# Gated outputs turned by block transposes on VectorE instead of 128x128 transposes on TensorE: one core, a hybrid GLA/HGRN2 layer

## The chip, the cores and the metric

The kernel runs on one core of one Trainium2 chip. The metric is device time in microseconds (us), the median of several runs. TensorE (PE in the profile; PEld is its weight load) does matmuls, VectorE (DVE) and ScalarE (ACT) elementwise work, GpSimd (POOL) a little of it, and SyncE (SP) issues nearly all transfers between main memory and the on-chip memory SBUF, each as one instruction on one in-order queue. In the text p is the time from one issue to the next on that queue for the small transfers that the change adds.

## The reference, cut to what matters

```python
p = jnp.einsum('btd,de->bte', h, w_in)                 # h: normalised, modulated x
...
o_a, s_a = chunked_gla(...)                            # 4 heads x 128 = 512 columns
o_h, s_h = chunked_gla(...)                            # 4 heads x 128 = 512 columns
o_a = rms_norm(o_a, g_on_gla).reshape(B, T, GLA_V) * jax.nn.silu(z_a)
o_h = rms_norm(o_h, g_on_hgrn).reshape(B, T, HGRN_W) * jax.nn.silu(z_h)
o = jnp.einsum('bte,ed->btd', jnp.concatenate([o_a, o_h], axis=-1), w_out)
y = x + gate[:, None] * rms_norm(o, g_post)
```

4096 prompt frames and 64 sample frames, model width 1024. The change touches only the way from `o_a` and `o_h` to the product with `w_out`.

## The kernel before, in words

The work is done in three stages. Stage one projects the frames for the GLA heads and runs their recurrence, group by group of 256 frames; stage two does the same for the HGRN2 heads. Both leave their normalised outputs in scratch memory, `oa_d` (already times its gate) and `oh_d` (not yet), one piece of 128 frames by 512 columns per tile. Stage three (`phase3`, from line 1218) has 33 tiles: 32 of 128 prompt frames and, as the seventh, one of 64 sample frames. For each tile it does the following.

- `load` (1229) fetches the two halves of the tile into `og` (two buffers) by `og_load` (1211), and the rows of x into `xt`, all on SP's queue.
- `turn` (1241) multiplies the second half by its gate `e` (1244; here called the gating), turns the tile by eight TensorE transposes of 128x128 (1252) into the PSUM tiles `ps_tp` and `ps_ms`, and splits the result by `split` (84) into a rounded part `ogh` on ScalarE (87) and a rest `ogl` on VectorE (88). The matmul needs frames along the free dimension and columns on the partitions, hence the turning.
- The output projection (1287) runs 48 matmuls of 512 columns: two output halves q, eight column blocks kt, three terms of hi and lo. The weights of kt 0 to 3 are tiles `wv`, those of kt 4 to 7 are `wu`.
- ScalarE squares the sum (1292), VectorE multiplies by the gate row (1296), does a Newton iteration for the reciprocal root (71 to 81, twelve tiny instructions), adds x (1299), and SP stores y (1303).

The gate `e` of a later tile comes from another projection, `z_tile` (1185): 24 matmuls (571) into `ps_at`, a sigmoid (1193) and a product (1194). A generator runs it some tiles ahead, so that 24 z matmuls stand beside the 48 of each output tile until the last five tiles, which have none. Its input `hf` is loaded by SP (527), four loads for two tiles, and split on ScalarE and VectorE (90, 91).

Within these, a scheduler in the framework sets the order on each engine when the program is built; an engine then runs its list in order. Every transfer has one of eight semaphores in turn, so that a transfer is issued only when the eighth before it has landed.

Of the kernel before, what the change touches and what calls it, by code (L numbers as in the profile page):

```python
# [6 lines left out]
F32 = mybir.dt.float32  # L7
# [4 lines left out]
ALU = mybir.AluOpType  # L12
# [3 lines left out]
P = 128  # L16
D = 1024
# [11 lines left out]
class Kernel:  # L29
# [1180 lines left out]

    def og_load(self, tile, og):

        g, j, (kind, _, r, _) = tile
        g = g if kind == "p" else -1
        self.nc.sync.dma_start(og[:r, :512], self.oa_d[g][j])
        self.nc.sync.dma_start(og[:r, 512:], self.oh_d[g][j])

    def phase3(self, tiles, zgen, og):
        nc, t = self.nc, self.t
        with ExitStack() as s:  # L1220
            one = self.pool(s, "p3one")
            ap = self.pool(s, "p3a")
            gg = one.tile([P, 2, D], F32, name="gg")
            for i in range(2):
                nc.sync.dma_start(gg[:, i, :], self.gate_d[i : i + 1, :].to_broadcast([P, D]))
            Wo = self.W3["o"]
            og0 = og

            def load(i):
                g, j, (kind, r0, r, o) = tiles[i]  # L1230
                if i > 0:
                    og = ap.tile([P, D], F32, name="og", bufs=2)
                    self.og_load(tiles[i], og)
                else:
                    og = og0
                xt = self.xp.tile([P, D], F32, name="xt", bufs=2)
                src = t["x_prompt"] if kind == "p" else t["x_sample"]
                nc.sync.dma_start(xt[:r], src[0, r0 : r0 + r, :])
                return og, xt

            def turn(i, og):
                r = tiles[i][2][2]
                e = self.zq.pop(0)
                nc.vector.tensor_tensor(og[:r, 512:], og[:r, 512:], e, ALU.mult)
                hi = ap.tile([P, D], F32R, name="ogh", bufs=2).rearrange("p (k c) -> p k c", k=KT)
                lo = None
                if r == P:
                    lo = ap.tile([P, D], F32R, name="ogl", bufs=2).rearrange("p (k c) -> p k c", k=KT)
                for q, tag in enumerate(("tp", "ms")):
                    pt = self.ps(tag).rearrange("p (k c) -> p k c", k=4)  # L1250
                    for k in range(4):
                        nc.tensor.transpose(
                            pt[:, k, :r], og[:r, (4 * q + k) * P : (4 * q + k + 1) * P], self.ident[:r, :r]
                        )
                    ks = slice(4 * q, 4 * q + 4)
                    self.split(hi[:, ks, :r], lo[:, ks, :r] if r == P else hi[:, ks, r : 2 * r], pt[:, :, :r], gain=self.col[:, 50 + q : 51 + q])
                return hi, lo

            n = len(tiles)
            og, xt = load(0)  # L1260
            next(zgen, None)
            hl = turn(0, og)
            for i in range(n):
                g, j, (kind, r0, r, o) = tiles[i]
                dst = t["y_prompt"] if kind == "p" else t["y_sample"]
                x_now, (hi, lo) = xt, hl
                if i + 1 < n:
                    next(zgen, None)
                    og, xt = load(i + 1)
                    hl = turn(i + 1, og)  # L1270
                cnd = 0 if kind == "p" else 1
                ss = self.small.tile([P, 2], F32, name="y_ss")[:r]
                y = ap.tile([P, D], F32, name="y", bufs=2)
                if i == n - 1:

                    self.tc.keep_in_program_order(nc.scalar.preload_act_table_set("natural_log_exp_and_others"))
                for q in range(2):
                    po = self.ps("pj")
                    cs = slice(512 * q, 512 * q + 512)
                    m = 0  # L1280
                    for kt in range(KT):
                        wh, wl = Wo[2 * kt + q][:, 0], Wo[2 * kt + q][:, 1]
                        if r < P:
                            self.pair_step(po, hi[:, kt, : 2 * r], r, wh, wl, kt)
                            continue
                        for a, b in ((hi, wh), (hi, wl), (lo, wh)):
                            nc.tensor.matmul(po[:r], a[:, kt, :r], b, start=m == 0, stop=m == 3 * KT - 1)  # L1287
                            m += 1
                    if r < P:
                        self.fold(po, r, 512, y[:, cs])  # L1290
                    junk = ap.tile([P, 512], mybir.dt.bfloat16, name="sq", bufs=1)[:r]
                    nc.scalar.activation(junk, po[:r], AF.Square, accum_out=ss[:, q : q + 1])  # L1292
                    if q:
                        nc.vector.tensor_tensor(ss[:, 0:1], ss[:, 0:1], ss[:, 1:2], ALU.add)
                        rs = self.rstd(ss[:, 0:1], D, table=i == n - 1)
                    nc.vector.tensor_tensor(y[:r, cs], po[:r], gg[:r, cnd, cs], ALU.mult)
                for q in range(2):
                    cs = slice(512 * q, 512 * q + 512)
                    nc.vector.scalar_tensor_tensor(y[:r, cs], y[:r, cs], rs, x_now[:r, cs], ALU.mult, ALU.add)
                    if i == n - 1:  # L1300
                        (nc.scalar if q else nc.sync).dma_start(dst[0, r0 : r0 + r, cs], y[:r, cs])
                if i < n - 1:
                    nc.sync.dma_start(dst[0, r0 : r0 + r, :], y[:r])
# [189 lines left out]
```

## Time and profile before

| what | us |
|---|---|
| median of 3 runs | 2168.07 (2166.62 to 2170.9) |
| profiled execution, own time | 2167.58 |
| profiled execution, span of the core | 2165.8 |
| PE busy in the span | 2121.3 (98%) |
| output tile with z matmuls, start to start | 17.30 |
| last matmul of stage three ends at | 2158.26 |

The times in the profile's rows run from the span's start. A row of the timeline reads: start, length, engine, line, operation, output<-inputs, count, and in brackets how long the engine had been idle before it and what ended that. SPq is SP's queue: the length is the time that the issuing instruction took, not the transfer's. A row of the chain of waits reads: start, length, engine, tile, line, count.

### The profile page before, as it was taken

What the parts mean: (1) busy time and instruction counts of PE and PEld (TensorE: products, weight loads), DVE (VectorE), ACT (ScalarE), POOL (GpSimd) and SP (SyncE); (2) the same over time, 40 slices, a digit from 0 to 9 for tenths busy, and PEclk for the clock granted to TensorE, in tenths of its full rate; (3) what the DMA queues carried; (4) which work ended last, traced back from release to release, by engine and by line L of the source; (5) the groups of instructions that cost most, each with busy time, mean ns of one, the idle gap of its engine ahead of it and who ended that gap; (6) DMA issues with size and microseconds to landing.
All of it is one profiled execution on the core that took longest, in us unless ns stands there. A gap on an engine that the chain in (4) does not pass through costs nothing.

```text
span 2165.8 us, 44469 instructions
## 1 busy us (share of the span) xinstructions
PE 2121.3 (98%) x16776; PEld 1868.9 (86%) x16776; DVE 1448.8 (67%) x4735; ACT 979.4 (45%) x2790; POOL 237.1 (11%) x636
## 2 busy tenths in 40 slices
PE   7999999999999999999999999999989999999998
PEld 6898899999999888889899988999868888888887
DVE  6866666666666687777778877677894454545444
ACT  5665555655556564434444444444542222222212
POOL 3200010000110111110111111000230000000000
PEclk9999999999999999999999999999999999999999
DMA  9321111211111231011121111001343433333322
GB/s 269 118 76 55 55 50 60 79 55 55 50 60 65 89 102 42 30 40 58 58 70 46 35 31 50 31 31 42 99 151 119 127 128 107 127 112 131 109 102 87
DMA packets 98706, 173.15 MB, mean 80 GB/s; under 512 B 12668, under 2 KB 34656, under 8 KB 98492
## 3 DMA queue, kind: packets, MB, share of 16 engines
q1 hardware_dynamic: 98348, 170.05, 24.1%
q8 instruction: 132, 2.16, 0.4%
q14 instruction: 82, 0.67, 0.1%
q10 hardware_dynamic: 144, 0.26, 0.0%
HBM read 118.35 MB, written 51.93 MB: 79 GB/s over the span
## 4 chain that ended last, share of the span: by engine, by line
PE 86%; DVE 7%; ACT 3%; DMA 3%; issue 1%; POOL 0%; SPq 0%; DVEq 0%; ACTq 0%; POOLq 0%
PE ps_pj L571 22%; PE ps_pj L559 22%; PE ps_pj L1287 16%; PE ps_at L571 7%; PE ps_at L908 2%; PE ps_ms L791 2%; PE ps_at L638 2%; PE ps_o L775 2%; PE ps_o L770 2%; DMA xt<-in_x_prompt_dram 2%; DVE wst L861 1%; PE ps_tp L506 1%; PE ps_at L718 1%; PE ps_tp L745 1%; PE ps_pj L579 1%
## 5 line engine op out<-in xcount | busy, mean ns | idle before, releaser
L571 PE MATMUL ps_pj<-wu,hh 128*128 128x512 f32 x1632 | 405.3, 397 | 3.3 <-DVE hh L91 2.4
L559 PE MATMUL ps_pj<-hh,wu 128*128 128x256 f32 (+1 forms) x2976 | 395.6, 287 | 0.0
L559 PEld LDWEIGHTS ps_pj<-hh,wu 128*128 128x128 f32 x2976 | 373.8, 191 | 4.6 <-issue 0.3
L571 PEld LDWEIGHTS ps_pj<-wu,hh 128*128 128x128 f32 x1632 | 297.6, 188 | 65.5 <-issue 3.5
L559 PE MATMUL ps_pj<-hh,wv 128*128 128x256 f32 (+1 forms) x1536 | 214.1, 289 | 0.0
L559 PEld LDWEIGHTS ps_pj<-hh,wv 128*128 128x128 f32 x1536 | 192.5, 188 | 14.9 <-issue 12.9
L571 PE MATMUL ps_pj<-wv,hh 128*128 128x264 f32 x1464 | 203.2, 290 | 1.6 <-DVE wv L91 1.6
L571 PEld LDWEIGHTS ps_pj<-wv,hh 128*128 128x128 f32 x1464 | 184.5, 188 | 6.5 <-issue 3.1
L1292 ACT ACTIVATE sq<-ps_pj 128x512 bf16<-128x512 f32 (+1 forms) x66 | 39.4, 597 | 294.7 <-PE ps_pj L1287 289.7
L1287 PE MATMUL ps_pj<-wv,ogh 128*128 128x512 f32 x512 | 163.0, 399 | 0.0
L571 PE MATMUL ps_at<-wu,hh 128*128 128x512 f32 x672 | 158.5, 392 | 0.0
L1287 PE MATMUL ps_pj<-wu,ogh 128*128 128x512 f32 x512 | 157.9, 390 | 0.0
L90 ACT CAST hh<-hf 128x512 fp32r<-128x512 f32 (+1 forms) x188 | 117.7, 626 | 75.2 <-PE ps_pj L571 36.8
L571 PEld LDWEIGHTS ps_at<-wu,hh 128*128 128x128 f32 x672 | 126.9, 189 | 26.4
L91 DVE TENSOR_TENSOR hh<-hf,hh 128x512 fp32r<-128x512 f32 (+1 forms) x188 | 133.1, 710 | 14.2 <-ACT hh L90 12.8
L1153 ACT ACTIVATE g<-ps_pj 128x256 f32<-128x256 f32 (+1 forms) x128 | 49.4, 386 | 198.2 <-PE ps_pj L559 197.7
L861 DVE TENSOR_TENSOR wst<-wst,T 128x160 f32<-128x160 f32 (+4 forms) x480 | 118.1, 263 | 4.0
L1287 PEld LDWEIGHTS ps_pj<-wu,ogh 128*128 128x128 f32 x512 | 96.1, 188 | 20.7
L890 POOL COPY T<-T 128x16 f32<-128x16 f32 (+1 forms) x32 | 9.6, 299 | 942.3 <-DVE Qg L831 870.4
L1287 PEld LDWEIGHTS ps_pj<-wv,ogh 128*128 128x128 f32 x512 | 94.4, 189 | 19.1
L1287 PE MATMUL ps_pj<-wv,ogl 128*128 128x512 f32 x256 | 100.7, 394 | 0.0
L1287 PE MATMUL ps_pj<-wu,ogl 128*128 128x512 f32 x256 | 99.7, 390 | 0.0
(300 smaller groups left out, 3705.7 us busy)
## 6 DMA issues: line engine op xcount, KB each, us to landing
xt<-in_x_prompt_dram SPq DMA_DIRECT2D x64, 512.0 KB
hf<-h_d SPq DMA_DIRECT2D x128, 256.0 KB
h_d<-hf SPq DMA_DIRECT2D x64, 256.0 KB
out_y_prompt_dram<-y SPq DMA_DIRECT2D x31, 512.0 KB
wst<-in_w_in_dram SPq DMA_DIRECT2D x36, 256.0 KB
ada_st<-in_w_ada_dram SPq DMA_DIRECT2D x32, 256.0 KB
oa_d<-e SPq DMA_DIRECT2D x32, 256.0 KB
oh_d<-e SPq DMA_DIRECT2D x32, 256.0 KB
```

The source lines that it names most:

```text
L90: self.nc.scalar.copy(hi, src)
L91: (eng or self.nc.vector).tensor_tensor(lo, src, hi.bitcast(F32), ALU.subtract)
L559: self.nc.tensor.matmul(ps[:, :T], a, b, start=i == 0, stop=i == n - 1)
L571: self.nc.tensor.matmul(ps[:r, : c1 - c0], a, b, start=kt == 0 and i == 0, stop=kt == KT - 1 and i == 2)
L638: nc.tensor.transpose(pt[:, i * P : (i + 1) * P], D[:, c + i, :], self.ident)
L770: nc.tensor.matmul(po[h], A[:, c * 4 + h, :], v, start=h < n, stop=St is None and h == 4 - n)
L775: nc.tensor.matmul(o, Q[rows[s], c * G + g, :], St[rows[s], g, :], start=NS == 2 and not apart and h == 1, stop=h == 4 - NS or h == 3 and ...
L791: nc.tensor.matmul(pd[s * w : (s + 1) * w, g, :], kc[:CL, g, s * w : (s + 1) * w], vs[c][:CL, h * P : (h + 1) * P], start=not apart, stop= ...
L861: nc.vector.tensor_tensor(parts(dst), parts(src), t.unsqueeze(3).to_broadcast(shape), ALU.mult)
L908: nc.tensor.matmul(pas[s][rows, g0 + g], K[rr, 2 * pr + g, rows], Yt[rr, o : o + P], start=True, stop=True)
L1153: nc.scalar.activation(sg, pf[:, :T], AF.Sigmoid)
L1287: nc.tensor.matmul(po[:r], a[:, kt, :r], b, start=m == 0, stop=m == 3 * KT - 1)
```

## The change

The tile is no longer turned by TensorE. Instead every half of it (512 columns) is loaded so that its columns already lie by quarters of partitions: partitions 32a to 32a+31 take the a-th group of 32 columns of every column block, 32 frames at a time. For one half that is 16 transfers of 32 partitions, 4 runs of 32 numbers (128 bytes) each, 16 KB in all. VectorE then transposes 32x32 blocks (`nc.vector.transpose`, STREAM_TRANSPOSE in the orders below), which completes the turn, and the split reads SBUF where it read PSUM.

The GLA half comes from main memory in this layout (16 loads for one before). The HGRN2 half is loaded as before, gated on VectorE, and then laid out by 16 more transfers from SBUF to SBUF into `oq`, half of a staging buffer (`wst`). `og` is loaded two tiles ahead, the gating stands in the middle of the tile before last, and the transposes one tile ahead. A 128-frame tile so has 32 small transfers and one ordinary one where it had two.

```diff
     def og_load(self, tile, og):
-        self.nc.sync.dma_start(og[:r, :512], self.oa_d[g][j])
+        src = self.oa_d[g][j].rearrange("(b t) (k a i) -> a b t k i", t=32, a=4, i=32)
+        for a in range(4):
+            for b in range(r // 32):
+                self.nc.sync.dma_start(self.quarter(og, a, b), src[a, b])
         self.nc.sync.dma_start(og[:r, 512:], self.oh_d[g][j])
+
+    @staticmethod
+    def quarter(t, a, b):
+        return t[32 * a : 32 * a + 32, b * P : b * P + P].rearrange("p (k i) -> p k i", i=32)
...
+            def gate(i, og):
+                r = tiles[i][2][2]
+                nc.vector.tensor_tensor(og[:r, 512:], og[:r, 512:], self.zq.pop(0), ALU.mult)
+                oq = self.wst()
+                for a in range(4):
+                    for b in range(r // 32):
+                        src = og[32 * b : 32 * b + 32, 512:].rearrange("p (k a i) -> p a k i", a=4, i=32)[:, a]
+                        nc.sync.dma_start(self.quarter(oq, a, b), src)
+                return og, oq
...
-                for q, tag in enumerate(("tp", "ms")):
-                    pt = self.ps(tag).rearrange("p (k c) -> p k c", k=4)
-                    for k in range(4):
-                        nc.tensor.transpose(
-                            pt[:, k, :r], og[:r, (4 * q + k) * P : (4 * q + k + 1) * P], self.ident[:r, :r]
-                        )
+                for q, src in enumerate(ogs):
                     ks = slice(4 * q, 4 * q + 4)
-                    self.split(hi[:, ks, :r], lo[:, ks, :r] if r == P else hi[:, ks, r : 2 * r], pt[:, :, :r], gain=self.col[:, 50 + q : 51 + q])
+                    oT = ap.tile([P, 512], F32, name="oT", bufs=1)[:, : 4 * r].rearrange("p (k c) -> p k c", k=4)
+                    nc.vector.transpose(
+                        oT.rearrange("p k (b t) -> p b k t", t=32),
+                        src[:, : 4 * r].rearrange("p (b k i) -> p b k i", k=4, i=32),
+                    )
+                    self.split(hi[:, ks, :r], lo[:, ks, :r] if r == P else hi[:, ks, r : 2 * r], oT, gain=self.col[:, 50 + q : 51 + q])
...
+            ogs = [gate(0, og)]
+            og = load(1)
+            hl = turn(0, ogs.pop(0))
+            next(zgen, None)
+            ogs.append(gate(1, og))
             for i in range(n):
                 if i + 1 < n:
                     next(zgen, None)
-                    og, xt = load(i + 1)
-                    hl = turn(i + 1, og)
+                    xt = load_x(i + 1)
+                    if i + 2 < n:
+                        og = load(i + 2)
+                    hl = turn(i + 1, ogs.pop(0))
...
+                    if q == 0 and i + 2 < n:
+                        ogs.append(gate(i + 2, og))
```

The order on SP's queue in the middle of stage three, before, two tiles (the last number of a scratch tile's name only numbers it; `oa_d_0_137` is the GLA half of a tile, `oh_d_0_139` its HGRN2 half):

```order
L1303 DMA out_y_prompt_dram<-y 128x1024
L1238 DMA xt<-in_x_prompt_dram 128x1024
L1215 DMA og<-oa_d_0_137 128x512
L1216 DMA og<-oh_d_0_139 128x512
L527 DMA hf<-h_d_151 128x512 x2
L1303 DMA out_y_prompt_dram<-y 128x1024
L1238 DMA xt<-in_x_prompt_dram 128x1024
L527 DMA hf<-h_d_151 128x512
```

And in the changed program, from the load of the same tile on:

```order
L1219 DMA og<-oa_d_0_137 32x4x32 x16
L1220 DMA og<-oh_d_0_139 128x512
L1332 DMA out_y_prompt_dram<-y 128x1024
L1245 DMA xt<-in_x_prompt_dram 128x1024
L1256 DMA wst<-og 32x4x32 x16
L1219 DMA og<-oa_d_1_138 32x4x32 x16
L1220 DMA og<-oh_d_1_140 128x512
L1332 DMA out_y_prompt_dram<-y 128x1024
L527 DMA hf<-h_d_156 128x512 x2
L1256 DMA wst<-og 32x4x32 x16
L527 DMA hf<-h_d_156 128x512 x2
```

Each tile's 16 transfers into `wst`, which wait for its gating, stand behind the loads of that very tile and ahead of the loads of the next.

On VectorE before, around the end of an output tile (1296 are its two halves out of PSUM, 1244 the gating of the next tile):

```order
L1296 TENSOR_TENSOR y<-ps_pj,gg 128x512
L1244 TENSOR_TENSOR og<-og,e 128x512
L1294 TENSOR_TENSOR y_ss<-y_ss 128x1
L1296 TENSOR_TENSOR y<-ps_pj,gg 128x512
L71 TENSOR_SCALAR y_ss<-y_ss 128x1
```

And after, with the numbers of the buffers (`y_23118` is one output tile; `og_22930` and `wst_22834` are the two halves of the next one; some rows of the Newton iteration are between the two pieces):

```order
L1325 TENSOR_TENSOR y_23118<-ps_pj_23119,gg_21801 128x512
L1323 TENSOR_TENSOR y_ss_23117<-y_ss_23117 128x1
L1325 TENSOR_TENSOR y_23118<-ps_pj_23165,gg_21801 128x512
L1269 STREAM_TRANSPOSE oT_23109<-og_22930 128x4x4x32
L1251 TENSOR_TENSOR og_22930<-og_22930,e_22296 128x512
...
L1328 SCALAR_TENSOR_TENSOR y_23118<-y_23118,nwt_y_23193,xt_22928 128x512 x2
L1269 STREAM_TRANSPOSE oT_23113<-wst_22834 128x4x4x32
L88 SCALAR_TENSOR_TENSOR ogl_23108<-oT_23113,col_168,ogh_23107 128x512
```

The gating of a tile now stands behind the last half of the tile before it, and both transposes of a tile stand there too, the second one behind the transfers that follow the gating.

On TensorE the eight transposes of each tile stood between the 24 z matmuls and the 48 of the tile:

```order
L571 MATMUL ps_at<-wu,hh 128x512 x24
L1252 MATMUL ps_tp<-ident,og 128x128 x4
L1252 MATMUL ps_ms<-ident,og 128x128 x4
L1287 MATMUL ps_pj<-wv,ogh 128x512 x2
L1287 MATMUL ps_pj<-wv,ogl 128x512
```

They are gone. The 48 are now split by halves of the turned tile, first the 24 of `wv` for both output halves, later the 24 of `wu`; in one tile of two all 24 z matmuls stand between the two halves, in the other 12 stand there and 12 ahead of the tile:

```order
L1314 MATMUL ps_pj<-wv,ogh 128x512 x2
L1314 MATMUL ps_pj<-wv,ogl 128x512
L571 MATMUL ps_at<-wu,hh 128x512 x24
L1314 MATMUL ps_pj<-wu,ogh 128x512 x4
L1314 MATMUL ps_pj<-wu,ogl 128x512
```

More of the change, by code (lines that the diff above doesn't have):

```diff
@@ L1226, in phase3, with load_x @@
             Wo = self.W3["o"]
-            og0 = og
             def load(i):
+                og = ap.tile([P, D], F32, name="og", bufs=2)
+                self.og_load(tiles[i], og)
+                return og
+            def load_x(i):
                 g, j, (kind, r0, r, o) = tiles[i]
[L1231 to L1235, printed above, removed]
                 xt = self.xp.tile([P, D], F32, name="xt", bufs=2)
@@ L1238, in load, with turn @@
                 nc.sync.dma_start(xt[:r], src[0, r0 : r0 + r, :])
-                return og, xt
-            def turn(i, og):
+                return xt
+            def gate(i, og):
                 r = tiles[i][2][2]
-                e = self.zq.pop(0)
-                nc.vector.tensor_tensor(og[:r, 512:], og[:r, 512:], e, ALU.mult)
+                nc.vector.tensor_tensor(og[:r, 512:], og[:r, 512:], self.zq.pop(0), ALU.mult)
[5 more added lines that the diff above has]
+                return og, oq
+            def turn(i, ogs):
+                r = tiles[i][2][2]
                 hi = ap.tile([P, D], F32R, name="ogh", bufs=2).rearrange("p (k c) -> p k c", k=KT)
@@ L1248, in turn @@
                     lo = ap.tile([P, D], F32R, name="ogl", bufs=2).rearrange("p (k c) -> p k c", k=KT)
-                for q, tag in enumerate(("tp", "ms")):
-                    pt = self.ps(tag).rearrange("p (k c) -> p k c", k=4)
-                    for k in range(4):
-                        nc.tensor.transpose(
-                            pt[:, k, :r], og[:r, (4 * q + k) * P : (4 * q + k + 1) * P], self.ident[:r, :r]
-                        )
-                    ks = slice(4 * q, 4 * q + 4)
-                    self.split(hi[:, ks, :r], lo[:, ks, :r] if r == P else hi[:, ks, r : 2 * r], pt[:, :, :r], gain=self.col[:, 50 + q : 51 + q])
+                for q, src in enumerate(ogs):
+                    ks = slice(4 * q, 4 * q + 4)
+                    oT = ap.tile([P, 512], F32, name="oT", bufs=1)[:, : 4 * r].rearrange("p (k c) -> p k c", k=4)
[3 more added lines that the diff above has]
+                    )
+                    self.split(
+                        hi[:, ks, :r], lo[:, ks, :r] if r == P else hi[:, ks, r : 2 * r], oT,
+                        gain=self.col[:, 50 + q : 51 + q],
+                    )
                 return hi, lo
             n = len(tiles)
-            og, xt = load(0)
+            xt = load_x(0)
             next(zgen, None)
-            hl = turn(0, og)
+            ogs = [gate(0, og)]
[3 more added lines that the diff above has]
+            ogs.append(gate(1, og))
             for i in range(n):
```

## The prediction

> **What bounds the kernel now.** I read the page first, for who is busy, then the chain of waits for the stage that the change touches, then the timelines of single queues for prices. The first rows of the page:
>
> ```profile
> span 2165.8 us, 44469 instructions
> PE 2121.3 (98%) x16776; PEld 1868.9 (86%) x16776; DVE 1448.8 (67%) x4735; ACT 979.4 (45%) x2790; POOL 237.1 (11%) x636
> PE 86%; DVE 7%; ACT 3%; DMA 3%; issue 1%; POOL 0%; SPq 0%; DVEq 0%; ACTq 0%; POOLq 0%
> ```
>
> PE is busy 98% of the span and makes up 86% of the chain that ends last; SP's queue makes up none of it. The chain of waits in stage three:
>
> ```profile
> 1742.86 10.98 PE ps_pj L1287 x48
> 1753.84 5.44 PE ps_at L571 x24
> 1760.16 10.98 PE ps_pj L1287 x48
> ...
> 2112.58 10.98 PE ps_pj L1287 x48
> 2124.44 10.99 PE ps_pj L1287 x48
> 2136.30 21.96 PE ps_pj L1287 x96
> ```
>
> A tile with z matmuls takes 1760.16-1742.86 = 17.30 us: 10.98 of output projection, 5.44 of z, and 0.88 between them (1753.84+5.44 = 1759.28 to 1760.16), in which the eight transposes run. Without z a tile is 2124.44-2112.58 = 11.86, again 10.98+0.88. The last matmul ends at 2136.30+21.96 = 2158.26, 7.54 before the span's end. Other resources in 100 us of this stage (columns: us, then busy time of PE, PEld, DVE, ACT, POOL, PEclk, DMA share, GB/s), and SP's queue in one tile of it:
>
> ```profile
> 1700.00:1800.00 100.00, 100.00 (x465) 81.70 (x464) 50.82 (x141) 26.55 (x56) 0.00 (x0) 1.00 0.37 121
> ```
> ```profile
> 1759.08 0.34 SPq L1303 DMA_DIRECT2D out_y_prompt_dram<-y  x1
> 1759.47 0.43 SPq L1238 DMA_DIRECT2D xt<-in_x_prompt_dram  x1
> 1760.19 0.55 SPq L1215 DMA_DIRECT2D og<-oa_d  x1
> 1760.79 0.47 SPq L1216 DMA_DIRECT2D og<-oh_d  x1
> 1773.99 1.78 SPq L527 DMA_DIRECT2D hf<-h_d  x2
> ```
>
> PE is full, DVE half idle, the DMA engines 37% busy, and SP issues six transfers in a round of 17.30.
>
> **The change: what it removes.** 33 tiles by 0.88 = 29.0 us of PE. If nothing else ended up on the path, the time would be 2167.58-29.0 = 2138.6.
>
> **What it adds on SP's queue.** 32 small transfers a tile, each an instruction on the in-order queue. The trace has none of this shape. The nearest rows: 64-row loads, a load with two runs a row (L529), and a group of four small loads:
>
> ```profile
> 1678.86 0.47 SPq L1215 DMA_DIRECT2D og<-oa_d  x1
> 1679.38 0.59 SPq L1216 DMA_DIRECT2D og<-oh_d  x1
> ```
> ```profile
> L529 SPq DMA_DIRECT2D hf<-h_s x8: 460/468/580, 792.6 to 1592.0; - x8
> ```
> ```profile
> 9.76 2.04 SPq L207 DMA_DIRECT2D ada_st<-in_w_ada_dram  x4
> 11.84 0.50 SPq L98 DMA_DIRECT2D e<-in_w_in_dram  x1
> ```
>
> From start to start, 0.04 to 0.06 is added to a length: 1678.86 to 1679.38 is 0.52, and the four take (11.84-9.76)/4 = 0.52. The second 64-row load gives 0.64. The two ordinary loads 1759.47 and 1760.79 give 0.43 to 0.47 and about 0.47 with the step. So p lies between 0.47 and 0.64; I take 0.55, nearest to the two 0.52 rows, since each of the transfers also waits for the one eight before it. 32p is then 17.6 us a tile, more than PE's whole 17.30-0.88 = 16.42.
>
> **What is serial.** In the order on SP's queue, the 16 transfers into `wst` of a tile wait for its gating, and the loads of the next tile stand behind them; the gating of that next tile waits for its `oh` load, which stands behind its 16 quarters. So from gating to gating run, one after another: 16p, 16p, the `oh` load, the gating. The loads' lead of two tiles doesn't open this ring. What an `oh` load takes with little beside it, and the gating:
>
> ```profile
> 2112.97 0.43 SPq L1216 DMA_DIRECT2D og<-oh_d  x1
> ```
> ```profile
> 2116.25 0.69 DVE L1244 TENSOR_TENSOR og<-og,e 128x512 f32<-128x512 f32 x1
> ```
>
> At most 2116.25-2112.97 = 3.28, and 0.69. The store of y, and x or half of the `hf` loads, issue while the `oh` load lands; every second round the remaining two `hf` and the x load stand in the ring, 3 by 0.47 = 1.41. Round: 32 by 0.55 + 3.28 + 0.69 = 21.57, every second one 22.98, mean 22.3, against PE's 16.42. That the queue binds is what I forecast.
>
> **The other chain, by DVE and PE.** The second transposes wait for the `wst` transfers, the gating stands behind both evictions of the tile before. Rows for an end of tile:
>
> ```profile
> 1760.38 0.69 ACT L87 ACTIVATE ogh<-ps_ms,col 128x512 fp32r<-128x512 f32 x1
> ...
> 1771.24 0.60 ACT L1292 ACTIVATE sq<-ps_pj 128x512 bf16<-128x512 f32 x1 [4.84 <-PE ps_pj L1287]
> ...
> 1772.03 0.69 DVE L1296 TENSOR_TENSOR y<-ps_pj,gg 128x512 f32<-128x512 f32 x1
> ```
> ```profile
> L1244 DVE TENSOR_TENSOR og<-og,e x32: 682/692/694, 1625.9 to 2116.3; 128x512 f32<-128x512 f32 x31, 64x512 f32<-64x512 f32 x1
> L1244 DVE TENSOR_TENSOR xt<-xt,e x1: 1755/1755/1755, 1601.4 to 1601.4; 128x512 f32<-128x512 f32 x1
> ```
> ```profile
> SPq L460 <- DMA xt<-gate_p: 1.3, 1, 1.3
> ```
>
> Last matmul to eviction done: 1772.72-(1760.16+10.98) = 1.58. DVE's transposes of 128x512 are in no trace: I take 0.69, the gating's of the same shape, with 1.76 (the same operation at its slowest) above. Twice 33 by 0.69 fits into DVE's idle half; only the two on the chain count. A quarter's landing lies between 1.3 (the wait for a tiny load) and the 3.28 above; I take 2.0, the nearer to the tiny one as 16 KB is a sixteenth of the `oh` load. Chain: 1.58 + 0.69 (transpose) + 0.69 (gating) + 16p + 2.0 + 0.69 (transpose) + 0.69 (rounding, ScalarE) + 24 matmuls, half of 10.98, = 11.83+16p = 20.6, every second one 22.0 with the 1.41 of other issues, mean 21.3. It is 1.0 below the ring at p = 0.55 and equal at p = 0.49; below that it binds. Free of p remains: eviction, transpose and rounding (2.96), then 24, 24 and 24 matmuls, 5.49+5.44+5.49, = 19.4, in the tiles whose z matmuls all stand between the halves.
>
> **The clock.** A row and two windows from the start of the stage:
>
> ```profile
> 1625.32 1.09 PE L1252 MATMUL ps_tp<-ident,og 128*128 128x128 f32 x4 [3.38 <-DMA og<-oa_d]
> ```
> ```profile
> 1620.00:1625.00 5.00, 1.94 (x9) 1.28 (x7) 3.72 (x7) 2.21 (x4) 0.00 (x0) 0.97 1.00 283
> 1625.00:1630.00 5.00, 4.68 (x19) 4.01 (x20) 1.44 (x2) 1.33 (x2) 0.00 (x0) 0.68 0.84 314
> ```
>
> After PE waited 3.38 the granted clock of the next 5 us was 0.68, 5 by 0.32 = 1.6 us lost. With 22.3-16.42 = 5.9 idle in each round this could return every tile; it lengthens the chain to 21.3+1.6 = 22.9, 0.6 over the ring. The Trainium skill, "TensorE: Matmul & The Clock Gate", section "Why this matters for your kernels", speaks against the change in the same way: idle gaps of more than about 3 us bring half clock back. By that rule the time would be that of the dear-clock rival below; the one gap here agrees with it.
>
> **The sum at p = 0.55.** The stage starts here:
>
> ```profile
> 1620.05 0.32 SPq L1109 DMA_DIRECT2D oh_d<-e  x1
> 1620.41 0.43 SPq L1215 DMA_DIRECT2D og<-oa_d  x1
> ```
>
> From 1620.4 the order has 6 transfers left of the first `wst` and 16 of the second tile's loads: 22 by 0.55 = 12.1, plus 3.97, gating of the second tile at 1636.5. 30 issues and 3.97 on (16.5+4.0), the third tile's is at 1657.0. From there to the gating of the 33rd are 30 rounds: 23 with z at 22.3 = 512.9, 7 without `hf` loads at 21.57 = 151.0, less 5 since the sample tile has half the transfers (its round is then PE's 17.3): 2315.9. Then the last 16 issues 8.8, landing 2.0, transpose and rounding 1.38, 24 matmuls 5.5: 2333.6, and 7.54 to the span's end: 2341.1. The profiled execution's own time is 1.78 above its span (2167.58-2165.8) and the median 0.49 above that: 2343.
>
> By the same sum, p = 0.64 gives rounds of 25.15 and 24.45: about 2432. At p = 0.47 the DVE chain binds (11.83+7.52+0.70 = 20.05, without `hf` 19.35): about 2271.
>
> **Rivals.**
>
> *The lead hides the issues (faster).* If the queue runs ahead, PE stays the bound: 2138.6. This decides at 32p + 3.97 + 0.70 below 16.42, so p below 0.37. For it: PE is full now and DMA is 37% busy, and transposes and loads are early in program order. Against it: ordinary issues take 0.43 and more, and the evictions ahead of the gating leave 2.96 of PE idle in every second tile, so that even then about half of the 0.88 is not gained. The Trainium skill has the rule for it in "DMA: Bandwidth & Descriptors", section "Issuing engines are not separate DMA queues": starting a DMA is usually small against the DMA itself. By that rule the time would be the 2138.6. The rows don't bear it out: 16 issues are 8.8, one landing at most 3.28. Chance 0.03.
>
> *Cheap issues, the chain by DVE binds.* At p = 0.42 (the length of a plain load alone) the chain is 11.83+6.72+0.70 = 19.25, the floor 19.4 in the other tiles: about 2250. For it: plain loads issue that fast. Chance 0.2.
>
> *Dear issues, or the clock.* p towards 0.64 (the second 64-row load), since many short runs may cost the issuer more: up to 2432; or the clock with 0.6 a round over 30 rounds, 19 us: 2362. Transposes at 1.76 belong here: two more on the chain by 2.1, 23.4 a round, 1.1 over the ring, 33 us: 2376. Chance 0.2.
>
> *The change doesn't do what it says.* The order shows the eight transposes gone from PE and all 32 transfers on SP; I give this none.
>
> **How the numbers follow.** The queue binds with p about 0.5 to 0.58: 0.57, predicted 2343. The range runs from 2260, between the sum at p = 0.47 and the cheap rival, to 2435, the sum at 0.64. Outside lie the first rival, half of the second and prices above 0.64, together some 0.2. Faster is the first rival alone, 0.03; within 0.2%, about what a measurement of this kernel can tell (the runs span 0.2%), 0.01, as no case ends there; slower 0.96.
>
> **What would show it.** Right: SP's queue is nearly without pauses in stage three; 32 transfers of 0.5 to 0.6 each; gating to gating about 22; PE's idle time named as waiting for `wst` or for ScalarE's rounding after it; PE down to some 70% there. Wrong: PE still full and the time below 2168 (the lead did hide it); SP pausing for DVE before each `wst` group (the chain by DVE binds); a landing beyond 4.4 (8 by 0.55), when each issue waits for the eighth before it; a granted clock below 0.9 throughout (the clock).

## The result, and the profile after

The changed kernel takes 2460.7 us (median of 4 runs, 2457.1 to 2462.6) against 2169.5 for the kernel before on the same chip: ratio 1.134, 95% interval 1.1326 to 1.1355. It is slower, as forecast, but by 291 us where 175 was forecast; 2460.7 lies above the range's upper end of 2435.

The first rows of the page after, and of its chain that ended last:

```profile
span 2459.0 us, 45147 instructions
PE 2197.3 (89%) x16512; PEld 1892.4 (77%) x16512; DVE 1498.8 (61%) x4801; ACT 987.8 (40%) x2790; POOL 237.1 (10%) x636
PE 54%; SPq 24%; DVE 8%; DMA 8%; issue 3%; ACT 2%; POOL 0%; DVEq 0%; ACTq 0%; POOLq 0%
```

SP's queue, which had no part of the chain, now has 24% of it, and PE has gone from 86% to 54%. 400 us of stage three, before and after (columns: us, then busy time of PE, PEld, DVE, ACT, POOL, PEclk, DMA share, GB/s):

```profile
1700.00:2100.00 400.00, 400.00 (x1852) 330.33 (x1851) 193.81 (x530) 99.07 (x209) 0.00 (x0) 1.00 0.35 115
```
```profile
1700.00:2100.00 400.00, 301.30 (x1106) 228.18 (x1105) 155.09 (x396) 74.45 (x146) 0.00 (x0) 0.88 0.36 91
```

PE stands idle a quarter of the time. Its clock is down to 0.88, and the DMA engines are no busier than before (0.36). What PE and DVE wait for, by the waits of the whole span (us in total, times, longest):

```profile
PE ps_pj L1314 <- ACT ogh L87: 216.2, 61, 6.9
```
```profile
DVE oT L1269 <- DMA wst<-og: 209.8, 29, 11.1
DVE oT L1269 <- DMA og<-oa_d: 75.7, 29, 10.5
DVE og L1251 <- DMA og<-oh_d: 22.3, 30, 1.1
```

PE waits for the rounded part, that one for the transpose, and the transpose for the small transfers. The last row is the gating: it waits for its `oh` load in 30 of 33 tiles, not for VectorE's own work before it. Two rounds on SP's queue (the timeline: start, length, count):

```profile
1909.62 0.59 SPq L1220 DMA_DIRECT2D og<-oh_d  x1
1910.31 0.38 SPq L1332 DMA_DIRECT2D out_y_prompt_dram<-y  x1
1910.78 1.50 SPq L527 DMA_DIRECT2D hf<-h_d  x2
1913.58 11.78 SPq L1256 DMA_DIRECT2D wst<-og  x16
1925.46 1.02 SPq L527 DMA_DIRECT2D hf<-h_d  x2
1926.53 0.42 SPq L1245 DMA_DIRECT2D xt<-in_x_prompt_dram  x1
1927.00 10.71 SPq L1219 DMA_DIRECT2D og<-oa_d  x16
1937.76 0.59 SPq L1220 DMA_DIRECT2D og<-oh_d  x1
1938.44 0.38 SPq L1332 DMA_DIRECT2D out_y_prompt_dram<-y  x1
1938.86 0.43 SPq L1245 DMA_DIRECT2D xt<-in_x_prompt_dram  x1
1941.91 10.26 SPq L1256 DMA_DIRECT2D wst<-og  x16
1952.21 11.03 SPq L1219 DMA_DIRECT2D og<-oa_d  x16
1963.29 0.59 SPq L1220 DMA_DIRECT2D og<-oh_d  x1
```

and two gatings between them on VectorE, with five pieces of the chain of waits in this window:

```profile
1941.19 0.69 DVE L1251 TENSOR_TENSOR og<-og,e 128x512 f32<-128x512 f32 x1 [1.00 <-DMA og<-oh_d]
...
1966.41 0.69 DVE L1251 TENSOR_TENSOR og<-og,e 128x512 f32<-128x512 f32 x1 [0.58 <-DMA og<-oh_d]
```
```profile
1912.86 0.69 DVE og L1251
...
1915.52 1.63 SPq L1256
...
1926.53 5.48 DMA xt<-in_x_prompt_dram
...
1932.02 0.54 SPq L1219
...
1957.35 1.39 SPq L1219
```

The ring of the prediction can be read off. From gating to gating, 1941.19 to 1966.41, are 25.22 us: gating and hand-over 0.72, sixteen issues 10.30 (1941.91 to 1952.21), sixteen more 11.08 (to 1963.29), the `oh` load till the next gating 3.12. The longer round before it, from 1912.86 (the chain's piece) to 1941.19, is 28.33: 0.72, 11.88, the other loads 1.54, 10.76, and 3.43. Sixteen issues without a hitch are 10.30, so 0.644 each. The excess of three of the four groups (1.58, 0.46, 0.78) lies in single issues. The one at 1932.02 waited for the x load, eight transfers before it, which landed 5.48 after its issue where eight small issues take 8 by 0.644 = 5.15. Those of 1.63 and 1.39 in place of 0.60 had a small transfer eight before them that had long landed; what made them long is open.

### The profile page after: what moved, and what is told of

Same layout as the page of the kernel before. It is cut to its first block, busy times and chain, and to the rows that moved or that the text cites. A ratio compares the mean times of both kernels' runs of the same rounds, so it can differ in the third digit from the quotient of the medians.

```text
span 2459.0 us, 45147 instructions
## 1 busy us (share of the span) xinstructions
PE 2197.3 (89%) x16512; PEld 1892.4 (77%) x16512; DVE 1498.8 (61%) x4801; ACT 987.8 (40%) x2790; POOL 237.1 (10%) x636
## 4 chain that ended last, share of the span: by engine, by line
PE 54%; SPq 24%; DVE 8%; DMA 8%; issue 3%; ACT 2%; POOL 0%; DVEq 0%; ACTq 0%; POOLq 0%
PE ps_pj L571 20%; PE ps_pj L559 19%; SPq L1256 13%; SPq L1219 11%; DMA og<-oh_d 4%; DMA xt<-in_x_prompt_dram 3%; PE ps_at L908 2%; PE ps_ms L791 2%; PE ps_at L638 2%; PE ps_o L775 2%; PE ps_o L770 2%; PE ps_at L718 1%; PE ps_tp L506 1%; DVE wst L861 1%; PE ps_tp L745 1%
## 5 line engine op out<-in xcount | busy, mean ns | idle before, releaser
L1314 PE MATMUL ps_pj<-wv,ogh 128*128 128x512 f32 x512 | 197.6, 484 | 110.3 <-ACT ogh L87 110.3
L1314 PE MATMUL ps_pj<-wu,ogh 128*128 128x512 f32 x512 | 182.8, 446 | 105.9 <-ACT ogh L87 105.9
L87 ACT ACTIVATE ogh<-oT,col 128x512 fp32r<-128x512 f32 (+1 forms) x66 | 47.2, 715 | 482.3 <-DVE oT L1269 434.8
L1314 PEld LDWEIGHTS ps_pj<-wv,ogh 128*128 128x128 f32 x512 | 119.7, 240 | 149.0 <-ACT ogh L87 122.5
L1314 PEld LDWEIGHTS ps_pj<-wu,ogh 128*128 128x128 f32 x512 | 108.3, 217 | 141.7 <-ACT ogh L87 119.5
L559 PEld LDWEIGHTS ps_pj<-hh,wv 128*128 128x128 f32 x1536 | 192.5, 188 | 14.9 <-issue 12.9
L1269 DVE STREAM_TRANSPOSE oT<-wst 128x512 f32<-128x512 f32 (+1 forms) x33 | 23.2, 703 | 232.7 <-DMA wst<-og 209.8
L1314 PE MATMUL ps_pj<-wv,ogl 128*128 128x512 f32 x256 | 113.2, 460 | 1.9 <-DVE ogl L88 1.7
L1325 DVE TENSOR_TENSOR y<-ps_pj,gg 128x512 f32<-128x512 f32 (+1 forms) x66 | 45.4, 687 | 108.3 <-ACT sq L1321 108.3
```

The costliest lines, as they stand in the source:

```text
L559: self.nc.tensor.matmul(ps[:, :T], a, b, start=i == 0, stop=i == n - 1)
```

## The experiments

Theory **Q** is the prediction's: SP's queue, at 0.64 us for each small transfer, in a ring from gating to gating. Rivals: **T**, the transfers themselves, whoever issues them; **C**, the chain through VectorE and TensorE; **K**, TensorE and its clock.

**GLA half alone.** The HGRN2 half is turned by TensorE again; its transfers go.

```diff
+if q == 1:
+    oT = self.ps("tp").rearrange("p (k c) -> p k c", k=4)[:, :, :r]
+    for k in range(4):
+        nc.tensor.transpose(oT[:, k, :], src[:r, k * P : k * P + P], self.ident[:r, :r])
+else:
     oT = ap.tile([P, 512], F32, name="oT", bufs=1)...   # DVE transpose
...
-        nc.sync.dma_start(self.quarter(oq, a, b), src)
```

> Only the GLA half comes by quarters and is turned on VectorE; the HGRN2 half is turned by four TensorE transposes again. Theory Q (SP's queue: 0.643 us for each small transfer, 32 of them in a ring from gating to gating) expects the ring to be gone: SP has 16 x 0.643 + about 3 for the six others = 13.3 us of work in a round, TensorE 17.30 - 0.44 = 16.86, so TensorE binds again and the time is 2169 - 33 x 0.44 = about 2155. Rival T (the transfers themselves, thousands of 128-byte runs a tile, load the DMA engines, whoever issues them) expects half of the excess: about 2169 + 145 = 2315. Rival C (the chain through VectorE: gating and transposes behind both evictions) expects TensorE idle by about 3 us in each tile: about 2220 to 2270.

Measured 2164.2 us (2158.1 to 2167.9, 10 runs), ratio 0.997, interval 0.996 to 0.9981. With half of the transfers not half but all of the excess is gone, which T does not give, and nothing is left of the 3 us a tile that C expects. Of the 14.5 that PE saves 6 arrive.

**HGRN2 half alone.** The mirror image: GLA loaded and turned as before, 16 transfers behind the gating.

> Only the HGRN2 half goes by quarters, from SBUF to SBUF behind its gating; the GLA half is loaded and turned on TensorE as before. Q expects about 2155, as for the GLA half alone: 16 small transfers a tile fit into TensorE's 16.86. T expects about 2315. C, the chain eviction, gating, 16 issues, landing, transpose, rounding, matmuls (11.83 + 10.3 = 22.1 a tile), expects about 2169 + 30 x 4.8 = 2313.

Measured 2196.7 (2195.1 to 2199.5), ratio 1.0129, interval 1.0114 to 1.0145. Neither number: far below T's and C's 2313, but 42 above Q's 2155. SP's timeline there:

```profile
1763.54 19.30 SPq L1254 DMA_DIRECT2D wst<-og  x28
1782.94 0.53 SPq L1335 DMA_DIRECT2D out_y_prompt_dram<-y  x1
1783.52 0.43 SPq L1243 DMA_DIRECT2D xt<-in_x_prompt_dram  x1
1783.99 2.77 SPq L1254 DMA_DIRECT2D wst<-og  x4
```

The queue's mean load fits, but its order does not: 28 small transfers of two tiles stand in one row of 19.30 us, and everything behind waits. PE was busy 380.5 of 400 us. The longest wait that the trace names for PE in this stage is 19.8 us in 13 waits, up to 5.1, for a PSUM bank that VectorE's rest `ogl` of the GLA half frees. In VectorE's order that `ogl` stands behind a transpose that itself waits for `wst` (6.65 us at 1776.38). So part of the loss goes over VectorE, as in C, though at far less than C's price. That a queue has room on average was not enough; which of the loads behind the row cost how much was not tried.

**The second 16 issued by ScalarE.** The whole change with another issuer.

```diff
-nc.sync.dma_start(self.quarter(oq, a, b), src)
+nc.scalar.dma_start(self.quarter(oq, a, b), src)
```

> The whole change, all 32 small transfers a tile, but the 16 behind the gating are issued from ScalarE's queue. Q expects the ring to open: SP has about 13.5 us a tile, ScalarE 10.3 + its own 4.5 = 14.8, TensorE 16.42; so near TensorE's bound, 2140 to 2180. T expects no change from 2460. C expects 22.1 a tile and 2313 or more, since the chain from gating to matmuls still holds 16 issues one after another.

Measured 2260.8 (2256.8 to 2262.5), ratio 1.0419, interval 1.0402 to 1.0436. The same transfers, 200 us less: T is out. It is also below C's 2313, but 80 above Q's upper 2180. ScalarE's timeline names the rest:

```profile
1916.83 7.96 ACTq L1256 DMA_DIRECT2D wst<-og  x10
1924.89 0.60 ACT L1321 ACTIVATE sq<-ps_pj 128x512 bf16<-128x512 f32 x1 [7.49 <-DMA wst<-og]
```

The square of an output half stands behind ten issues, the eviction waits for the square, and PE for the bank (57.7 us in 19 waits): here an engine that computes is a poor place for a row of issues.

**Other shapes, same number and bytes.** (Not the transposed layout, so the output is another; the 64-frame tile keeps the old shapes.)

```diff
-self.nc.sync.dma_start(self.quarter(og, a, b), src[a, b])
+c = 128 * a + 32 * b
+self.nc.sync.dma_start(og[:, c : c + 32], self.oa_d[g][j][:, c : c + 32])
...
-nc.sync.dma_start(self.quarter(oq, a, b), src)
+nc.sync.dma_start(oq[32 * a : 32 * a + 32, b * P : b * P + P], og[32 * b : 32 * b + 32, 512 + 128 * a : 640 + 128 * a])
```

> As many transfers of as many bytes, but in other shapes (the layout is then not the transposed one, so the output is not the reference's): the GLA loads are 128 partitions by one run of 128 bytes, the SBUF to SBUF ones 32 partitions by one run of 512 bytes. If the issue's price comes from fewer than 128 partitions, the first shape goes at 0.43 to 0.47 from start to start and the second stays at 0.64; if from the four runs a partition, both go at 0.43 to 0.47. Q expects the round to fall by 16 times what each shape saves: 2.7 us for one shape (about 2380), 5.4 for both (about 2300).

The two lines by source (count, then shortest/median/longest ns of the issuing instruction):

```profile
L1223 SPq DMA_DIRECT2D og<-oa_d x496: 319/430/1995, 1627.6 to 2353.3; - x166
L1261 SPq DMA_DIRECT2D wst<-og x496: 507/589/1557, 1638.9 to 2367.0; - x166
```

128 partitions by one run: 0.43; 32 partitions by one run: 0.59, against 0.60 with four runs. From SBUF the number of runs hardly matters. From main memory 128 partitions by one run cost less than 32 by four, but there partitions and runs changed together, so which of the two sets the price is not shown. One run of the kernel gave 2387, Q's "about 2380" for one cheap shape of two.

**More TensorE work.** Each z projection is computed twice, 24 more matmuls in a round.

```diff
+for _ in range(2):
     for _ in self.proj_tok(pz, self.W3["z"], 0, 512, h, o, r):
         yield
```

> Every z projection is computed twice into the same bank (the second overwrites the first), 24 more matmuls, 5.44 us, in each of 30 rounds; all else is the whole change. The order changes with it: SP's transfers into the staging buffer and the loads of the next tile are mixed, so that the ring from gating to gating is partly open. Theory Q expects that the added 163 us of TensorE work costs nothing, as SP still has 32 x 0.643 + about 3.4 = 24 us a tile and TensorE 21.9: 2380 to 2460. A rival by which TensorE or its clock is on the path (K) expects up to 2460 + 163 = 2620; the clock granted should rise to near 1.

Measured 2411.6 (2408.1 to 2415.1), ratio 1.1122, interval 1.1101 to 1.1142: 163 us of work more, 49 us less time. K does not fit that. The order changed as well, so the run is no test of the work alone. The same 400 us now read

```profile
1700.00:2100.00 400.00, 375.12 (x1576) 303.09 (x1575) 157.05 (x422) 70.86 (x157) 0.00 (x0) 0.96 0.38 96
```

with PE busy 375 and the clock at 0.96. By the trace the gain is the order's: a round on SP,

```profile
1914.40 0.59 SPq L1221 DMA_DIRECT2D og<-oh_d  x1
1915.03 3.94 SPq L1220 DMA_DIRECT2D og<-oa_d  x5
1919.07 8.33 SPq L1257 DMA_DIRECT2D wst<-og  x13
...
1937.76 0.59 SPq L1221 DMA_DIRECT2D og<-oh_d  x1
```

is 23.36 with hardly a pause (23.96 on average over thirty rounds), so that the `oh` load and gating no longer add to the issues. Opening the ring alone leaves the sum of the issues as the bound.

**x and hf loads issued by GpSimd.**

```diff
-nc.sync.dma_start(xt[:r], src[0, r0 : r0 + r, :])
+nc.gpsimd.dma_start(xt[:r], src[0, r0 : r0 + r, :])
...                                   # the hf loads of stage three likewise
```

> The whole change, but the loads of x and hf are issued by GpSimd, so that SP has only the 32 small transfers, the oh load and the store of y, and its eight transfers in flight are small ones. In the order of SP three of the 16 quarter loads then issue while the oh load lands. Q expects a round of 29 x 0.643 + 0.69 + 3.4 = 22.8 instead of 26.8 in the 23 rounds with hf, less in the others: 2340 to 2370. If the waits for the slots of large loads and their issues are not what makes a round longer than 25.15, the time falls only by the 3 x 0.643: about 2400.

Measured 2388.1 (2385.5 to 2390.8), ratio 1.1013. Two gatings on VectorE:

```profile
1939.01 0.69 DVE L1253 TENSOR_TENSOR og<-og,e 128x512 f32<-128x512 f32 x1 [0.92 <-DMA og<-oh_d]
1962.29 0.69 DVE L1253 TENSOR_TENSOR og<-og,e 128x512 f32<-128x512 f32 x1
```

A round of 23.28 here (23.08 on average over thirty), near the forecast 22.8, and 73 us less in all. The time missed 2340 to 2370 because the expectation took 26.8, the mean of the two rounds above, for all; over all thirty the mean of the changed kernel is 25.53. The 2.4 a round are, by the rows, two or three quarter issues that now go while the `oh` load lands (1.3 to 1.9), the 1.54 of large loads in every second round with z, and little else. So the slots that x and `hf` hold are a small part.

**The second 16 issued by GpSimd,** as on ScalarE, with `nc.gpsimd`.

> The whole change, with the 16 transfers behind the gating issued by GpSimd, which does nothing else in this stage; so no engine that computes has issues in its queue. On ScalarE (2261) TensorE waited for the eviction, which waited for ScalarE's square behind 16 issues. Q with issues at SP's price expects 10.3 us a tile on GpSimd, 13.5 on SP and TensorE's 16.42: 2140 to 2165. If GpSimd's issue costs above 1.0 us, it becomes the bound: 16 us at 1.0, 32 us and above 2600 at 2.0. Rival C expects no better than the 2261.

Measured 2165.5 (2157.7 to 2176.7, 10 runs), ratio 0.9982, interval 0.9967 to 0.9998. All 32 transfers are there, the layout and VectorE's work too, and the 291 us are gone. C at its price is out: it gave no better than 2261. Q's range holds at its upper edge only: of the 29.0 us that PE saves, 3.5 arrive. The waits that the trace names for PE in this stage (6.2 us for evictions, 5.9 for `ogl`) explain part of the rest. GpSimd's issues and the stretch:

```profile
L1256 POOL DMA_DIRECT2D wst<-og x504: 548/548/558, 1639.7 to 2140.1; - x168
```
```profile
1700.00:2100.00 400.00, 386.58 (x1678) 315.18 (x1676) 210.29 (x586) 99.38 (x212) 212.04 (x392) 0.99 0.52 134
```

**GLA half alone, in loads of 128 partitions.** By frame block and column block.

```diff
-for a in range(4):
-    for b in range(r // 32):
-        self.nc.sync.dma_start(self.quarter(og, a, b), src[a, b])
+src = self.oa_d[g][j].rearrange("(b t) (k a i) -> b k a t i", t=32, a=4, i=32)
+for b in range(r // 32):
+    for k in range(4):
+        self.nc.sync.dma_start(og[:, b * P + 32 * k : b * P + 32 * k + 32], src[b, k])
```

> Only the GLA half by small loads, as in the run that gave 2164, but each load covers all 128 partitions by one run of 128 bytes (by frame block and column block instead of by frame block and quarter): same number, same bytes, same layout, correct. The price measured for that shape is 0.475 from start to start against 0.643, so SP has 7.6 + 3 us a tile instead of 10.3 + 3. If SP's queue still costs in the 2164 version (its best is 2155), this gains 3 to 9 us; if it doesn't, no difference: 2164.

Measured 2154.0 (2152.7 to 2157.4), ratio 0.9932, interval 0.9919 to 0.9946: all of the 14.5 us of four transposes a tile, so the loads' old shape did still cost in the 2164 version (whose best was 2158.1, not the 2155 of the expectation). That it cost through SP's queue is argued, from the price of an issue: the two profiled executions, of 2158.1 and 2157.4, are too close to show it. 2154.0 is the fastest median here. PE is full again:

```profile
L1219 SPq DMA_DIRECT2D og<-oa_d x504: 500/508/2497, 1622.7 to 2115.1; - x168
```
```profile
1700.00:2100.00 400.00, 400.00 (x1802) 328.05 (x1801) 208.38 (x579) 101.16 (x212) 0.00 (x0) 1.00 0.43 120
```

**Both:** those loads on SP, the second 16 on GpSimd.

> The whole change with what the runs so far found cheap: the GLA loads each over all 128 partitions (0.475 on SP), the 16 transfers behind the gating from GpSimd (about 0.54 each there). Q expects SP at 7.6 + 3.4 = 11, GpSimd at 8.7, TensorE at 16.42 a tile, so TensorE's bound, 2140, if its waits for evictions go too; at worst the 2165 that GpSimd alone gave. Rival C (a chain from gating to the second transposes, 16 issues, holds it whatever the queue) expects no better than 2165.

Measured 2156.7 (2150.9 to 2163.0), ratio 0.9936, interval 0.9921 to 0.9951. Below the 2165, but not 2140. In its best stretch PE is full at a tile of 16.40 (chain of waits, then the window):

```profile
1873.68 10.97 PE ps_pj L1314 x48
1884.64 5.44 PE ps_at L571 x24
1890.08 10.97 PE ps_pj L1314 x48
```
```profile
1700.00:2100.00 400.00, 390.33 (x1693) 319.07 (x1692) 213.52 (x594) 100.75 (x216) 213.80 (x396) 0.99 0.52 134
```

Elsewhere it loses 9.7 of 400 us (the profiled execution is the slowest of the six, with a span of 2161.2). Which wait starts these slips is open. With 12.6 us gained it is no better than the GLA half alone.

## Why the prediction was wrong, point by point

- **PE's saving, 0.88 a tile: right.** 1884.64+5.44 = 1890.08 leaves nothing between z and projection in the last run, and the half change got its half.
- **The ring on SP binds: right**, in its place and order, and by the runs that moved issues off SP (2165, 2261) against those that left them (2388, 2412). In the changed kernel the gatings waited for the `oh` load.
- **p = 0.55: wrong, the step that failed.** It measured 0.644. It was set by the rows with an equal start-to-start step, 0.52; the row that came true was the second 64-row load, 0.59+0.05, which the prediction had as the range's upper end only. The first 64-row load, of the same shape, took 0.47, so the rows did not say which to follow. The reason that was given for dear issues, many short runs, is not borne out: from SBUF one run cost 0.59 and four cost 0.60. Nor is shape all: the ordinary `oh` load, 0.47 before, takes 0.59 in the rows above, straight behind 16 small loads. What sets the price is open. 32 by 0.094 = 3.0 a round.
- **Single hitches: a term left out.** From the third tile's gating at 1663.92 to the last at 2429.79 thirty rounds took 765.9 us, forecast 658.9: 107 more. 944 small transfers by 0.094 make 89 of it. The rest is counted in the trace: 19 issues longer than 0.75 cost 12.9 beyond 0.60, pauses for a slot held by x or `hf` 4.5 (the prediction weighs the eight slots for small transfers alone), smaller pauses 2.4. Together that is 109, so the account closes to about 2 us. The third gating came 6.9 late, 4.9 of it by p (52 issues). The end took 4.0 more, 1.5 of it by p and 2.3 in the last matmuls at a granted clock of 0.72 (the last piece of the chain):

```profile
2443.92 7.75 PE ps_pj L1314 x24
```

  107+6.9+4.0 = 118 is the whole miss, and about 95 of it is p (89+4.9+1.5).
- **Landing 2.0, transpose 0.69, `oh` load 3.28: right.** A quarter from SBUF landed in 1.85 (median over the trace's semaphores), the `oh` load in 3.25 (median; 2.8 to 3.4), and the transposes:

```profile
L1269 DVE STREAM_TRANSPOSE oT<-wst x33: 438/712/712, 1628.3 to 2442.4; 128x512 f32<-128x512 f32 x32, 128x256 f32<-128x256 f32 x1
```

- **The chain by DVE, 11.83+16p: not tested as priced.** At 0.644 it would be 22.1, under the ring. It is no fixed floor: with the issues on two queues the order on TensorE changed too (all 24 z matmuls between tiles), and tiles of 16.42 came.
- **The clock: present, but not on the path.** It fell to 0.88, and with it at 0.96 the round still followed SP; it shows in the time only in the last matmuls. The rule of the Trainium skill, "TensorE: Matmul & The Clock Gate", section "Why this matters for your kernels", that idle gaps of more than about 3 us bring half clock back, agrees with the 0.88 beside PE's waits of up to 6.9 us.
- **The rival that the lead hides the issues:** false here, where one issue is 0.60 and the ring holds all. With two queues the excess goes, but of the 29.0 only 3.5 are gained, or 12.6 with the wider loads. The rule of the Trainium skill, "DMA: Bandwidth & Descriptors", section "Issuing engines are not separate DMA queues", that starting a transfer is usually small beside the transfer, does not hold for these: one issue took 0.60 beside a landing of 1.85, a third of it, and 16 issues in a row took 10.30.

The first signs held (hardly a pause outside the ring's own waits, 0.60 an issue, rounds above 22, PE at 75%). One of the signs of being wrong came as well, a granted clock below 0.9, but it was no cause. The range failed at its upper end, since p = 0.64 gave 2432 there without the hitches and the late clock.

## What to carry to other kernels

Before work is turned into many small transfers, multiply their number by the dearest issue of a like shape in the trace and set it against the round of the engine that binds; bytes and DMA share say nothing about it. Then follow the in-order queue once around: what waits on it, what stands behind, and add something for single issues that hang. Wider shapes (all 128 partitions), and an issuer that computes nothing, can make the same layout pay, here by 12.6 of 2169 us.

## What the hardware showed unexpectedly

- In a row of its like an issue on SP took 0.43 us for 128 partitions by one run of 128 bytes, 0.51 for 128 partitions from a source in three dimensions, 0.59 to 0.60 for 32 partitions, with one run (from SBUF) or four.
- The issue before counts too: the ordinary `oh` load, 128 partitions by one run of 2 KB, took 0.59 in every tile straight behind 16 small loads, and 0.47 at the median in the kernel before.
- About one issue in fifty on SP took 0.79 to 1.67 us with no wait that the trace shows (19 of 944 above 0.75), most of them 50 to 75 transfers apart; the cause is open.
- GpSimd's issue of the same 32-partition transfer took 0.548 with hardly any scatter, less than SP's.
